# A hybrid gated-mixer block in fp32 on one core: which engine makes the sums of weight quarters

## The chip, the core and the metric

The kernel runs on one core of a Trainium2 chip. Five engines work side by side, each through its own list of instructions in order: TensorE (PE; its weight loads are shown apart as PEld), VectorE (DVE), ScalarE (ACT), GpSimd (POOL) and SyncE (SP). SP issues plain loads. POOL issues loads that add: a DMA that adds what it reads from memory to what lies in a tile. The metric is device microseconds of one execution. The kernel before took 719.77 us (median of 3, 717.58 to 720.23).

## The reference

For x of 512 x 1024, one layer:

```
h = rmsnorm(x, norm_g);  proj = h @ w_in             # w_in: 1024 x 12288
a_u,a_v,a_z, b_p,b_z, c_h,c_b,c_c,c_z, g0,g1,g2 = split(proj, 1024 columns each)
ya = spatial_gating(gelu(a_u), gelu(a_v)) * silu(a_z)
yb = multiscale_pool(b_p) * silu(b_z)                # windows 2, 4, 8, 16, then pool_w
yc = c_b * causal_conv(c_c * c_h, width 3) * silu(c_z)
merged = sum over i of sigmoid(g_i) * (y_i @ w_branch_i)     # three, 1024 x 1024 each
out = rmsnorm(x + merged @ w_out)
```

All of it is in fp32. Almost all the work is in the matrix products with w_in, the three w_branch and w_out.

## The kernel before, in words

**Operands.** Every fp32 operand of a matmul is split in two parts that TensorE multiplies at full rate: ScalarE casts it (`whi`, line 61), VectorE subtracts the cast from it (`wlo`, line 62). Three matmuls (hi·hi, hi·lo, lo·hi) make one product. A tile of weights is 128 x 1024 elements, 512 KB; there are 7 buffers of raw weights (`wraw`), 4 of `whi`, 4 of `wlo`, 2 for a sum that is made by DMA (`wsum`, called `s1`).

**Seven products in place of eight.** A weight block is cut in four quarters and the activations in four too; a scheme of Strassen's kind needs seven products of quarters. For that some operands are sums of weight quarters, and some are sums of activation quarters (`t1` to `t4`, made once at the start; b11, b21, b22 are quarters).

**Groups.** Of the 24 blocks of 512 columns of `w_in`, two are made plainly at the start (line 120 on), and 22 are *groups* (function `group`): two groups for each of the other eleven outputs (`ch`, `cb` and so on; `g` is 0 or 1). A group makes 7 products of 24 matmuls of 256 columns, in the order b11, b21, t2, t1, t3, b22, t4. Its sums of weights: `s1` is one quarter loaded by SP plus another added by POOL (line 460); a11−a21, s1−a11 and a12−(the new a11) are VectorE's (line 448), the second and third each built on an earlier one. `copied` moves a result bank to SBUF (ScalarE), `plus` adds two partial results (VectorE, line 445). The last two products of a group, b22 and t4, are issued after the first product of the next group (`run`, from line 492).

**Projections.** `merge` makes two gate groups and then the projection of a branch: 7 products of 48 matmuls (line 645). Four of its operands lie in turn in one *chain tile*: a quarter, to which POOL adds three more quarters one after the other (`w.add`), each after the product that read the value before it; a fifth load and a fourth adding DMA make `s3`. The output projection (from line 909) is built alike, with matmuls of 512 columns (line 874).

**Order.** A scheduler of the tile framework reorders the instructions of each engine by its own estimate of when operands are ready; so an engine's order isn't that of the code. A buffer is used again when all that reads it is done. Between the groups stand the mixing steps of branch a (line 549), the pooling of branch b (line 747 and `pool_mm`), and the convolution of branch c (ScalarE line 833, VectorE lines 834 and 836), which reads `cc` and stands inside the next group, `cb`.

Of the kernel before, what the change touches and what calls it, by code (L numbers as in the profile page):

```python
# [11 lines left out]
ALU = mybir.AluOpType  # L12
# [4 lines left out]
S = 512  # L17
# [7 lines left out]
PAD = 16  # L25
# [5 lines left out]
def mixers_kernel(ctx, tc, x, norm_g, w_in, sgu_ln_g, sgu_ln_b, sgu_w, sgu_b, pool_w, pool_b, pool_scale,  # L31
# [24 lines left out]
    def bank():  # L56
        return psum.tile([P, 512], F32, tag="ps", name="ps")
# [271 lines left out]
    b11, b12, b22, b21 = hsum  # L329
    moving = {"b11": hq[0, 0], "b21": hq[1, 0], "b22": hq[1, 1]}  # L330

    def sum_form(name, tag, out, in0, in1):
        nc.vector.tensor_tensor(out=out, in0=in0, in1=in1, op=ALU.subtract)
        moving[name] = form_tile(name, tag)
        split(*moving[name], out)


    sum_form("t1", "f3", b11, b12, b11)
    sum_form("t3", "f4", b12, b22, b12)
    sum_form("t2", "f5", b22, b22, b11)  # L340


    ws_bs = outs.tile([P, 2, KT, P], F32, tag="outs", name="ws_bs")
# [45 lines left out]
        nc.vector.tensor_scalar(out=v_t[:, b, :], in0=v_t[:, b, :], scalar1=mv[:, 0:1], scalar2=rv,  # L389
                                op0=ALU.subtract, op1=ALU.mult)  # L390

    sum_form("t4", "f6", b21, b21, b22)

    def proj(w, j, rhs_hi, rhs_lo, nk=KT):
        ps = bank()
# [18 lines left out]
    def pair_of(ap):  # L414
        return ap.rearrange("p (j t) -> p j t", j=2)

    def group(c0, g, ct, use=None):
        def source(kh, nh):
            c = c0 + nh * HALF + g * GC
            return w_in[kh * HALF : (kh + 1) * HALF, c : c + GC].rearrange("(k p) c -> p k c", p=P)  # L420

        def quarter(kh, nh):
            return load_raw(source(kh, nh), [4, GC])

        def halved(raw):
# [12 lines left out]

        def copied(ps):
            s = part.tile([P, S], F32, tag="part", name="part")  # L440
            nc.scalar.copy(out=s, in_=ps)
            return pair_of(s)

        def plus(half, ts, s, ps):
            nc.vector.tensor_tensor(out=ct[:, half, :, ts], in0=pair_of(ps), in1=s, op=ALU.add)  # L445

        def sub(out, in0, in1, op=ALU.subtract):
            nc.vector.tensor_tensor(out=out, in0=in0, in1=in1, op=op)  # L448

        a11 = quarter(0, 0)  # L450
        f = halved(a11)
        px, py, pz = bank(), None, None
        product(f, "b11", px, True)
        yield
        c1 = copied(px)
        a12 = quarter(1, 0)
        f = halved(a12)
        s1 = wsum.tile([P, 4, GC], F32, tag="wsum", name="s1")
        nc.sync.dma_start(out=s1, in_=source(0, 1))
        nc.gpsimd.dma_start(out=s1, in_=source(1, 1), accum_op=ALU.add)  # L460
        a21, a22 = quarter(0, 1), quarter(1, 1)
        py = bank()
        product(f, "b21", py, True)
        plus(0, T1, c1, py)
        sub(a21, a11, a21)
        sub(a11, s1, a11)
        product(halved(a11), "t2", px, False)
        c2 = copied(px)
        pz = bank()
        product(halved(s1), "t1", pz, True)  # L470
        product(halved(a21), "t3", px, False)
        c3 = copied(px)
        sub(a12, a12, a11)
        plus(1, T2, c3, pz)
        yield
        product(halved(a12), "b22", pz, False)
        plus(0, T2, c2, pz)
        if use:
            use(ct[:, 0], 0, slice(0, S))
            use(ct[:, 1, :, T2], 1, T2)  # L480
        product(halved(a22), "t4", px, False)
        if use:
            use(pair_of(px), 1, T1)
        else:
            nc.scalar.copy(out=ct[:, 1, :, T1], in_=pair_of(px))
        yield

    def run(items):
# [21 lines left out]
                    after()  # L510
        finish()

    def act_into(ct, func):
        def use(src, half, ts):
            nc.scalar.activation(out=ct[:, half, :, ts], in_=src, func=func)
        return use

    def y_tile():
# [78 lines left out]
    class Weights:  # L597
# [17 lines left out]
    def parts(raws):  # L615
# [5 lines left out]
            units.append((hi, lo))  # L621
        return units

    def banks():
        return [bank() for _ in range(2)]


    def merge(br, w_branch):
# [49 lines left out]
        def projection():  # L678
            q, w = Quarters(y, home), Weights(w_branch)
            w11 = w.plain(0, 0)  # L680
            px, py = banks(), banks()
            product(w11, q.form("b11"), px, True)
            c1 = copied(px, tile512)
            yield
            chain = w.add(w.plain(1, 0), 1, 1)
            product(w.plain(0, 1), q.form("b21"), py, True)
            under(0, T1, py, c1)
            pz = banks()
            product(chain, q.form("-t1"), pz, True)
            z5 = copied(pz, tile512)  # L690
            w.add(chain, 0, 0)
            product(chain, q.form("-t2"), px, False)
            s3 = w.add(w.plain(0, 0), 1, 0)
            w.add(chain, 0, 1)
            c2 = copied(px, part512)
            product(s3, q.form("t3"), px, False)
            under(1, T2, px, z5, -1.0)
            yield
            product(chain, q.form("b22"), pz, False)
            under(0, T2, pz, c2)  # L700
            product(w.plain(1, 1), q.form("-t4"), px, False)
            under(1, T1, px, None, -1.0)
            yield
# [108 lines left out]
    def branch_c(g):  # L812
        c = {}

        def part_of(name, off, func=None):
            c[name] = out_tile(name)
            yield from group(OFF[off], g, c[name], act_into(c[name], func) if func else None)

        def conv_in():
            c["cc"] = out_tile("cc")  # L820

            def use(src, half, ts):
                nc.vector.tensor_mul(out=pads[half][:, :, PAD + ts.start : PAD + ts.stop], in0=src,
                                     in1=c["ch"][:, half, :, ts])
# [13 lines left out]

        def gate_in():
            c["cb"] = out_tile("cb")  # L840

            def use(src, half, ts):
                y1 = c["cc"][:, half, :, ts]
                nc.vector.tensor_mul(out=y1, in0=src, in1=y1)
# [68 lines left out]
    product(w.plain(0, 0), q.form("b11"), px, True)  # L913
    chain = w.add(w.plain(1, 0), 1, 1)
    product(chain, q.form("-t1"), pz, True)
    w12 = w.plain(0, 1)
    w.add(chain, 0, 0)
# [5 lines left out]
    s3 = w.add(w.plain(0, 0), 1, 0)  # L923
    w.add(chain, 0, 1)
# [4 lines left out]
    product(s3, t3, px, False)  # L929
    w22 = w.plain(1, 1)  # L930
    product(chain, q.form("b22"), pz, False)
# [29 lines left out]
```

## Time and profile before

| | |
|---|---|
| three runs | 717.58, 719.77, 720.23 us |
| the profiled execution | 721.86 us; its span 720.1 us, mean granted TensorE clock 0.983 |
| busy share of the span | PE 95%, PEld 91%, DVE 81%, ACT 53%, POOL 11% |
| HBM read | 118.00 MB, 167 GB/s over the span |
| adding DMAs by POOL (queue software_dynamic) | 28.32 MB |

TensorE is busy nearly throughout, so what can be won or lost in time stands at the few places where it isn't. Its matmuls overlap: one of 256 columns lasts 0.28 us by its row and the next begins 0.117 us later, so time is counted by the distance of their starts. The stages, by the span's clock: start and the first two blocks of `w_in` up to some 99 us, the mixing steps near 100 and 144 us, projection a at 219 to 260, b at 376 to 421, c at 600 to 661, and from there the output projection.

### The profile page before, as it was taken

Reading aid. Unit: us, or ns where it says so; the run is one execution under the profiler, and the core shown is the slowest. Engines: PE = TensorE matmul, PEld = TensorE weight load, DVE = VectorE, ACT = ScalarE, POOL = GpSimd, SP = SyncE. Lnnn points to the kernel's source line nnn. Section 1 sums busy time; section 2 is a strip of 40 time slices with the busy share of each in tenths; the row PEclk is TensorE's granted clock in tenths of the full one; section 3 lists DMA queues with packets and bytes.
Section 4 is the critical chain, followed back from the end, with each engine's and each line's share of the span. In section 5 each row is a group of like instructions: output and inputs, shape, how many; then the busy total and the mean of one; then the engine's idle time right before and its main releaser. Section 6 shows DMA issues by size and latency. Waiting matters only on the chain.

```text
span 720.1 us, 12691 instructions
## 1 busy us (share of the span) xinstructions
PE 684.0 (95%) x5246; PEld 654.7 (91%) x5246; DVE 581.2 (81%) x674; ACT 380.4 (53%) x464; POOL 82.4 (11%) x92
## 2 busy tenths in 40 slices
PE   8999999989998899999998999999999999989694
PEld 6779999989998899999998899999999999989563
DVE  6998678599787798995867797897779896779596
ACT  6544555546454554765764434646445465565253
POOL 3112000000122001000122000000000001212101
PEclk9999999999999999999999999999999999999988
DMA  7964436616689736557598547465666627978833
GB/s 267 326 139 118 147 88 176 176 52 184 177 234 181 180 123 159 149 147 201 139 256 154 151 142 187 151 161 159 150 155 194 176 91 219 244 171 234 184 60 117
DMA packets 96478, 120.93 MB, mean 168 GB/s; under 512 B 3804, under 2 KB 73508, under 8 KB 96420
## 3 DMA queue, kind: packets, MB, share of 16 engines
q1 hardware_dynamic: 75508, 90.75, 39.1%
q0 software_dynamic: 20320, 28.32, 24.0%
q10 hardware_dynamic: 592, 1.05, 0.4%
q8 instruction: 41, 0.67, 0.4%
q14 instruction: 17, 0.14, 0.1%
HBM read 118.00 MB, written 2.10 MB: 167 GB/s over the span
## 4 chain that ended last, share of the span: by engine, by line
PE 69%; DMA 12%; DVE 10%; issue 5%; ACT 2%; POOL 1%; SPq 0%; POOLq 0%; DVEq 0%; ACTq 0%
PE ps L435 53%; PE ps L645 6%; DMA wraw<-in_w_in 4%; DVE wlo L62 3%; PE ps L874 3%; DMA wraw<-in_w_branch_a 3%; DMA wraw<-in_w_branch_b 3%; PE ps L256 2%; DVE win L747 1%; PE ps L97 1%; PE ps L98 1%; PE ps L96 1%; ACT whi L61 1%; DMA wraw<-in_w_out 1%; DMA wraw<-in_w_branch_c 1%
## 5 line engine op out<-in xcount | busy, mean ns | idle before, releaser
L61 ACT CAST whi<-wraw 128x1024 fp32r<-128x1024 f32 (+1 forms) x192 | 199.3, 1041 | 256.1 <-PE ps L435 140.2
L62 DVE TENSOR_TENSOR wlo<-wraw,whi 128x1024 fp32r<-128x1024 f32 (+1 forms) x192 | 231.2, 1210 | 95.4 <-ACT whi L61 95.0
L645 PE MATMUL ps<-yl,whi 128*128 128x256 f32 x336 | 96.6, 288 | 6.4 <-DVE yl L62 6.4
L645 PE MATMUL ps<-yh,wlo 128*128 128x256 f32 x336 | 96.8, 289 | 4.7 <-DVE wlo L62 4.7
L645 PE MATMUL ps<-yh,whi 128*128 128x256 f32 x336 | 96.4, 287 | 0.7 <-ACT yh L61 0.7
L460 POOL DMA_DIRECT2D s<-in_w_in x22 | 28.8, 1310 | 390.1 <-DMA s<-in_w_in 81.3
L645 PEld LDWEIGHTS ps<-yl,whi 128*128 128x128 f32 x336 | 65.3, 194 | 7.2 <-DVE yl L62 7.2
L645 PEld LDWEIGHTS ps<-yh,wlo 128*128 128x128 f32 x336 | 65.5, 195 | 6.1 <-DVE wlo L62 6.1
L645 PEld LDWEIGHTS ps<-yh,whi 128*128 128x128 f32 x336 | 65.4, 195 | 1.1 <-ACT yh L61 1.1
L448 DVE TENSOR_TENSOR wraw<-wraw 128x1024 f32<-128x1024 f32 x44 | 53.5, 1218 | 13.9 <-DMA wraw<-in_w_in 13.8
L435 PE MATMUL ps<-b22h,whi 128*128 128x256 f32 x176 | 51.5, 292 | 3.7 <-DVE sz L445 3.7
L435 PE MATMUL ps<-b22l,whi 128*128 128x256 f32 x176 | 50.0, 284 | 0.0
L435 PE MATMUL ps<-b22h,wlo 128*128 128x256 f32 x176 | 49.8, 283 | 0.0
L435 PE MATMUL ps<-b11l,whi 128*128 128x256 f32 x176 | 49.6, 282 | 0.0
L435 PE MATMUL ps<-t2l,whi 128*128 128x256 f32 x176 | 49.5, 281 | 0.0
L435 PE MATMUL ps<-t1l,whi 128*128 128x256 f32 x176 | 49.5, 281 | 0.0
L435 PE MATMUL ps<-t3l,whi 128*128 128x256 f32 x176 | 49.5, 281 | 0.0
L435 PE MATMUL ps<-b21l,whi 128*128 128x256 f32 x176 | 49.5, 281 | 0.0
L435 PE MATMUL ps<-t4l,whi 128*128 128x256 f32 x176 | 49.5, 281 | 0.0
L435 PE MATMUL ps<-b11h,whi 128*128 128x256 f32 x176 | 49.3, 280 | 0.0
L435 PE MATMUL ps<-t3h,whi 128*128 128x256 f32 x176 | 49.3, 280 | 0.0
L435 PE MATMUL ps<-b21h,whi 128*128 128x256 f32 x176 | 49.3, 280 | 0.0
(243 smaller groups left out, 2002.6 us busy)
## 6 DMA issues: line engine op xcount, KB each, us to landing
wraw<-in_w_in SPq DMA_DIRECT2D x96, 512.0 KB, 4.7
s<-in_w_in SPq DMA_DIRECT2D x22, 512.0 KB, 3.6
s<-in_w_in POOLq DMA_DIRECT2D x22, 512.0 KB, 6.0
wraw<-in_w_branch_a SPq DMA_DIRECT2D x10, 512.0 KB, 6.2
wraw<-in_w_branch_b SPq DMA_DIRECT2D x10, 512.0 KB, 7.2
wraw<-in_w_branch_c SPq DMA_DIRECT2D x10, 512.0 KB, 3.6
wraw<-in_w_out SPq DMA_DIRECT2D x10, 512.0 KB, 8.6
wraw<-in_w_branch_a POOLq DMA_DIRECT2D x8, 512.0 KB, 8.2
```

What stands on the lines that cost most here:

```text
L61: keep(nc.scalar.copy(out=hi, in_=src))
L62: keep(nc.vector.tensor_tensor(out=lo, in0=src, in1=hi.bitcast(F32), op=ALU.subtract))
L96: nc.tensor.matmul(ps, lhsT=a[0], rhs=b[0], start=first, stop=False)
L97: nc.tensor.matmul(ps, lhsT=a[0], rhs=b[1], start=False, stop=False)
L98: nc.tensor.matmul(ps, lhsT=a[1], rhs=b[0], start=False, stop=last)
L256: pin(nc.tensor.matmul(vps[b], lhsT=a, rhs=r, start=done[b] == 1, stop=done[b] == 3 * KT))
L435: nc.tensor.matmul(ps[:, j * GC : (j + 1) * GC], lhsT=a[x][:, k, j * P : (j + 1) * P], rhs=moving[b][y][:, k, :], start=first and j == 0 a ...
L448: nc.vector.tensor_tensor(out=out, in0=in0, in1=in1, op=op)
L460: nc.gpsimd.dma_start(out=s1, in_=source(1, 1), accum_op=ALU.add)
L645: nc.tensor.matmul(ps, lhsT=units[k // 2][x_][:, k % 2, j * P : (j + 1) * P], rhs=form[y_][:, k, :], start=first and j % 2 == 0 and k == 0 ...
L747: nc.vector.tensor_add(out=nxt[:, lo:], in0=cur[:, lo:], in1=cur[:, lo - step : PAD + S - step])
L874: nc.tensor.matmul(pss[b], lhsT=m[x_][:, k, b * P : (b + 1) * P], rhs=units[k // 2][y_][:, k % 2, :], start=first and k == 0 and n == 0, s ...
```

## The change

In a group the products stand in the order b11, b21, −t1, −t2, t3, b22, −t4. The tile `s1` is the operand of −t1 and then, with a11 added to it by VectorE (line 472), of −t2. The tile a11 gets a quarter added by a POOL DMA (line 473) and is the operand of t3. a12 gets `s1` added by VectorE (line 477). No separate tile a21 is loaded; four of six loads stay plain and two add, where it was five and one. The activation sums −t1, −t2 and −t4 have their signs turned, and the operations that read their results take the sign in.

In the projections the chain tile gets one adding DMA, `w11` a second one (two quarters each), and VectorE makes the other two sums (`sum_onto`, line 638 of the changed file), one operation for each half tile. The fifth load and `s3` are gone.

```
def group(...):                     # cut
         a11 = quarter(0, 0)
         product(f, "b11", px, True)
         c1 = copied(px)
-        a12 = quarter(1, 0)
-        f = halved(a12)
         s1 = wsum.tile([P, 4, GC], F32, tag="wsum", name="s1")
         nc.sync.dma_start(out=s1, in_=source(0, 1))
         nc.gpsimd.dma_start(out=s1, in_=source(1, 1), accum_op=ALU.add)
-        a21, a22 = quarter(0, 1), quarter(1, 1)
+        a12 = quarter(1, 0)
+        f = halved(a12)
         py = bank()
         product(f, "b21", py, True)
         plus(0, T1, c1, py)
-        sub(a21, a11, a21)
-        sub(a11, s1, a11)
-        product(halved(a11), "t2", px, False)
-        c2 = copied(px)
-        pz = bank()
-        product(halved(s1), "t1", pz, True)
-        product(halved(a21), "t3", px, False)
+        pz = bank()
+        product(halved(s1), "-t1", pz, True)
+        nc.vector.tensor_tensor(out=s1, in0=s1, in1=a11, op=ALU.add)
+        nc.gpsimd.dma_start(out=a11, in_=source(0, 1), accum_op=ALU.add)
+        product(halved(s1), "-t2", px, False)
+        c2 = copied(px)
+        a22 = quarter(1, 1)
+        nc.vector.tensor_tensor(out=a12, in0=a12, in1=s1, op=ALU.add)
+        product(halved(a11), "t3", px, False)
         c3 = copied(px)
-        sub(a12, a12, a11)
-        plus(1, T2, c3, pz)
+        plus(1, T2, c3, pz, 1.0 if use else -1.0)
         yield
         product(halved(a12), "b22", pz, False)
...
+    def sum_onto(raws, others):
+        for a, b in zip(raws, others):
+            nc.vector.tensor_tensor(out=a, in0=a, in1=b, op=ALU.add)
...
def projection():                   # cut
             chain = w.add(w.plain(1, 0), 1, 1)
-            product(w.plain(0, 1), q.form("b21"), py, True)
-            under(0, T1, py, c1)
+            w12 = w.plain(0, 1)
             pz = banks()
             product(chain, q.form("-t1"), pz, True)
+            sum_onto(chain, w11)
+            w.add(w11, 1, 0)
             z5 = copied(pz, tile512)
-            w.add(chain, 0, 0)
+            py = banks()
+            product(w12, q.form("b21"), py, True)
+            under(0, T1, py, c1)
             product(chain, q.form("-t2"), px, False)
-            s3 = w.add(w.plain(0, 0), 1, 0)
-            w.add(chain, 0, 1)
             c2 = copied(px, part512)
-            product(s3, q.form("t3"), px, False)
+            sum_onto(w12, chain)
+            product(w11, q.form("t3"), px, False)
             under(1, T2, px, z5, -1.0)
             yield
-            product(chain, q.form("b22"), pz, False)
+            product(w12, q.form("b22"), pz, False)
```

The output projection changes in the same way. The orders of the engines move with it; three places follow, before and then after. A name's number tells its tile.

VectorE in the first group after projection b (`ch`, g = 0), from the split of its first tile on, before: `pr` and `merged` belong to the projection, `s1_4644` is the group's `s1`, `wraw_4605` its a11, `wraw_4638` its a12, `wraw_4647` its a21, `part` a copied bank.

```order
L62 TENSOR_TENSOR wlo_4608<-wraw_4605,whi_4607 128x1024
L62 TENSOR_TENSOR wlo_4641<-wraw_4638,whi_4640 128x1024
L661 TENSOR_TENSOR pr_4597<-ps_4053,gate_3537 128x512
L448 TENSOR_TENSOR wraw_4605<-s1_4644,wraw_4605 128x1024
L662 TENSOR_TENSOR merged_2472<-merged_2472,pr_4597 128x2x256
L661 TENSOR_TENSOR pr_4600<-ps_4054,gate_3883 128x512
L62 TENSOR_TENSOR wlo_4680<-wraw_4605,whi_4679 128x1024
L662 TENSOR_TENSOR merged_2472<-merged_2472,pr_4600 128x2x256
L62 TENSOR_TENSOR wlo_4711<-s1_4644,whi_4710 128x1024
L62 TENSOR_TENSOR wlo_4739<-wraw_4647,whi_4738 128x1024
L445 TENSOR_TENSOR ch_4604<-ps_4651,part_4636 128x2x256
L448 TENSOR_TENSOR wraw_4638<-wraw_4638,wraw_4605 128x1024
```

The same place after: `s1_4606` is `s1`, `wraw_4573` a11, `wraw_4609` a12, `wraw_4737` the a11 of the next group.

```order
L62 TENSOR_TENSOR wlo_4612<-wraw_4609,whi_4611 128x1024
L678 TENSOR_TENSOR merged_2529<-merged_2529,pr_4565 128x2x256
L677 TENSOR_TENSOR pr_4568<-ps_4026,gate_3857 128x512
L62 TENSOR_TENSOR wlo_4643<-s1_4606,whi_4642 128x1024
L678 TENSOR_TENSOR merged_2529<-merged_2529,pr_4568 128x2x256
L472 TENSOR_TENSOR s1_4606<-s1_4606,wraw_4573 128x1024
L477 TENSOR_TENSOR wraw_4609<-wraw_4609,s1_4606 128x1024
L451 TENSOR_TENSOR ch_4572<-ps_4615,part_4604 128x2x256
L62 TENSOR_TENSOR wlo_4673<-s1_4606,whi_4672 128x1024
L62 TENSOR_TENSOR wlo_4706<-wraw_4573,whi_4705 128x1024
L62 TENSOR_TENSOR wlo_4740<-wraw_4737,whi_4739 128x1024
L62 TENSOR_TENSOR wlo_4769<-wraw_4609,whi_4768 128x1024
```

The split of `s1` (for −t1) now stands ahead of the sum into `s1`; the split of a11 (for t3, `wraw_4573`) stands behind it and behind a DMA, and the split of the next group's first tile right behind that one.

VectorE in the first `cb` group, around the convolution, before: `ppad` is its padded input, lines 834 and 836 the convolution, `wraw_4995` the group's s1−a11 (t2), `s1_5106` its t1, `wraw_5109` its t3.

```order
L62 TENSOR_TENSOR wlo_5142<-wraw_4995,whi_5141 128x1024
L448 TENSOR_TENSOR wraw_5335<-wraw_5233,wraw_5335 128x1024
L445 TENSOR_TENSOR cc_4770<-ps_4933,part_4931 128x2x256
L62 TENSOR_TENSOR wlo_5173<-s1_5106,whi_5172 128x1024
L823 TENSOR_TENSOR ppad0_1780<-cc_4770,ch_4604 128x2x512
L823 TENSOR_TENSOR ppad1_1782<-ps_4777,ch_4604 128x2x256
L62 TENSOR_TENSOR wlo_5201<-wraw_5109,whi_5200 128x1024
L834 SCALAR_TENSOR_TENSOR cc_4770<-ppad0_1780,pvec_451,cc_4770 128x512 x2
L836 SCALAR_TENSOR_TENSOR cc_4770<-ppad0_1780,pvec_451,cc_4770 128x512 x2
L834 SCALAR_TENSOR_TENSOR cc_4770<-ppad1_1782,pvec_451,cc_4770 128x512 x2
L836 SCALAR_TENSOR_TENSOR cc_4770<-ppad1_1782,pvec_451,cc_4770 128x512 x2
L445 TENSOR_TENSOR cb_4994<-ps_5113,part_5098 128x2x256
```

The same place after: `s1_5064` holds −t1's operand up to line 472 and −t2's from there, and lines 851 and 853 are the convolution.

```order
L472 TENSOR_TENSOR s1_5064<-s1_5064,wraw_4959 128x1024
L477 TENSOR_TENSOR wraw_5067<-wraw_5067,s1_5064 128x1024
L451 TENSOR_TENSOR cc_4736<-ps_4863,part_4922 128x2x256
L523 SCALAR_TENSOR_TENSOR ppad1_1772<-ps_4743,ch_4572 128x2x256
L521 TENSOR_TENSOR ppad0_1770<-cc_4736,ch_4572 128x2x512
L851 SCALAR_TENSOR_TENSOR cc_4736<-ppad1_1772,pvec_451,cc_4736 128x512 x2
L851 SCALAR_TENSOR_TENSOR cc_4736<-ppad0_1770,pvec_451,cc_4736 128x512 x2
L853 SCALAR_TENSOR_TENSOR cc_4736<-ppad0_1770,pvec_451,cc_4736 128x512 x2
L853 SCALAR_TENSOR_TENSOR cc_4736<-ppad1_1772,pvec_451,cc_4736 128x512 x2
L451 TENSOR_TENSOR cb_4958<-ps_5073,part_5062 128x2x256
L62 TENSOR_TENSOR wlo_5131<-s1_5064,whi_5130 128x1024
L62 TENSOR_TENSOR wlo_5164<-wraw_4959,whi_5163 128x1024
```

Three splits of the group stood ahead of the convolution; now the two sums stand ahead of it, and the splits of −t2 and t3 behind it.

TensorE at the end of −t2 in the first `ch` group, after (`ps_4579` is the group's bank, `ps_4743` one of the next group, 12 matmuls of which stand here):

```order
L439 MATMUL ps_4579<--t2h_442,whi_4672 128x256
L439 MATMUL ps_4579<--t2l_443,whi_4672 128x256
L439 MATMUL ps_4579<--t2h_442,wlo_4673 128x256
L439 MATMUL ps_4743<-b11h_169,whi_4739 128x256
L439 MATMUL ps_4743<-b11l_170,whi_4739 128x256
L439 MATMUL ps_4743<-b11h_169,wlo_4740 128x256
```

And the end of those 12 matmuls:

```order
L439 MATMUL ps_4743<-b11h_169,whi_4739 128x256
L439 MATMUL ps_4743<-b11l_170,whi_4739 128x256
L439 MATMUL ps_4743<-b11h_169,wlo_4740 128x256
L439 MATMUL ps_4579<-t3h_437,whi_4705 128x256
L439 MATMUL ps_4579<-t3l_438,whi_4705 128x256
```

Before, t2, t1 and t3 of one group followed each other; the border of t1 and t3 (`ps_4709` is the other bank of the group):

```order
L435 MATMUL ps_4709<-t1h_432,whi_4710 128x256
L435 MATMUL ps_4709<-t1l_433,whi_4710 128x256
L435 MATMUL ps_4709<-t1h_432,wlo_4711 128x256
L435 MATMUL ps_4611<-t3h_437,whi_4738 128x256
L435 MATMUL ps_4611<-t3l_438,whi_4738 128x256
L435 MATMUL ps_4611<-t3h_437,wlo_4739 128x256
L435 MATMUL ps_4611<-t3h_437,whi_4738 128x256
```

After, matmuls of the next group's b11 stand ahead of t3, so that TensorE reaches that tile's split before t3's.

## Rows read from the trace of the kernel before

**Rows 1.** The page's first part: busy us (share of the span) and instructions.

```profile
PE 684.0 (95%) x5246; PEld 654.7 (91%) x5246; DVE 581.2 (81%) x674; ACT 380.4 (53%) x464; POOL 82.4 (11%) x92
```

**Rows 2.** Windows: us, PE, PEld, DVE, ACT, POOL busy (x), PEclk, DMA share, GB/s.

```profile
99.10:106.00 6.90, 6.15 (x52) 5.96 (x52) 6.90 (x12) 2.01 (x3) 0.00 (x0) 1.00 0.01 2
143.51:153.50 9.99, 7.21 (x50) 7.02 (x50) 8.88 (x13) 2.74 (x3) 0.26 (x2) 0.83 0.01 3
218.78:259.82 41.04, 36.68 (x290) 35.67 (x289) 30.39 (x33) 18.62 (x22) 4.80 (x4) 0.96 0.71 168
376.21:421.46 45.25, 40.19 (x316) 38.92 (x315) 35.79 (x42) 19.36 (x23) 4.80 (x4) 0.96 0.63 150
600.00:661.00 61.00, 58.68 (x485) 58.27 (x484) 44.45 (x49) 33.30 (x39) 10.80 (x9) 0.97 0.89 223
660.90:710.60 49.70, 41.73 (x170) 31.94 (x168) 39.83 (x51) 21.47 (x32) 8.15 (x7) 0.93 0.53 115
500.00:520.00 20.00, 20.00 (x171) 19.86 (x170) 16.24 (x16) 9.90 (x12) 1.29 (x1) 1.00 0.61 160
```

**Rows 3.** The chain of waits: start us, us, engine and what.

```profile
136.80 7.73 DMA wraw<-in_w_in
...
673.93 8.89 DMA wraw<-in_w_out
...
694.74 13.49 PE ps L874 x57
```

**Rows 4.** Windows, after the wait of projection a.

```profile
248.00:252.00 4.00, 4.00 (x22) 4.00 (x23) 3.48 (x6) 0.00 (x0) 0.00 (x0) 0.57 0.61 171
```

**Rows 5.** Waits: engine, line, waited for: us in total, times, longest us.

```profile
ACT whi L61 <- DMA wraw<-in_w_branch_a: 9.4, 3, 7.9
...
DVE wraw L448 <- DMA wraw<-in_w_in: 3.2, 1, 3.2
...
PE ps L874 <- ACT mh L61: 7.1, 1, 7.1
```

**Rows 6.** Groups by form: busy, mean ns of one, idle before.

```profile
L62 DVE TENSOR_TENSOR wlo<-wraw,whi 128x1024 fp32r<-128x1024 f32 x188 | 228.5, 1221 | 94.2 <-ACT whi L61 93.8
L61 ACT CAST whi<-wraw 128x1024 fp32r<-128x1024 f32 x188 | 196.8, 1050 | 250.1 <-PE ps L435 134.2 <-issue 32.0 <-PE ps L645 20.7
...
L448 DVE TENSOR_TENSOR wraw<-s,wraw 128x1024 f32<-128x1024 f32 x22 | 26.9, 1221 | 0.3
```

**Rows 7.** DMA issues: KB each, median us to landing; then line 460 alone.

```profile
s<-in_w_in SPq DMA_DIRECT2D x22, 512.0 KB, 3.6
s<-in_w_in POOLq DMA_DIRECT2D x22, 512.0 KB, 6.0
...
wraw<-in_w_branch_a POOLq DMA_DIRECT2D x8, 512.0 KB, 8.2
...
DMA to landing us min/median/max: 5.5/6.0/11.8
```

**Rows 8.** Timeline of VectorE: start us, us, engine, line, operation.

```profile
464.00 1.41 DVE L834 SCALAR_TENSOR_TENSOR cc<-ppad,pvec,cc 128x512 f32<-128x512 f32 x2
...
469.90 3.49 DVE L62 TENSOR_TENSOR wlo<-wraw,whi 128x1024 fp32r<-128x1024 f32 x3
```

**Rows 9.** Timeline of TensorE and ScalarE at a product's end.

```profile
441.06 0.28 PE L435 MATMUL ps<-t4h,wlo 128*128 128x256 f32 x1
...
441.26 1.05 ACT L61 CAST whi<-wraw 128x1024 fp32r<-128x1024 f32 x1 [1.67 <-PE ps L435]
...
442.21 0.58 ACT L485 COPY ch<-ps 128x512 f32<-128x512 f32 x1
```

**Rows 10.** Timeline of VectorE and POOL, projection a.

```profile
218.00 1.22 DVE L62 TENSOR_TENSOR wlo<-wraw,whi 128x1024 fp32r<-128x1024 f32 x1
...
219.53 1.19 POOL L612 DMA_DIRECT2D wraw<-in_w_branch_a  x1 [2.77 <-DVE wlo L62]
```

**Rows 11.** Timeline of ScalarE, the convolution's activations.

```profile
462.38 2.94 ACT L833 ACTIVATE cc<-ppad,pvec 128x512 f32<-128x512 f32 x4
```

More of the change, by code (lines that the diff above doesn't have):

```diff
@@ L330, in mixers_kernel, with sum_form @@
     moving = {"b11": hq[0, 0], "b21": hq[1, 0], "b22": hq[1, 1]}
-    def sum_form(name, tag, out, in0, in1):
-        nc.vector.tensor_tensor(out=out, in0=in0, in1=in1, op=ALU.subtract)
+    def sum_form(name, tag, out, in0, in1, sign=1.0):
+        if sign == 1.0:
+            nc.vector.tensor_tensor(out=out, in0=in0, in1=in1, op=ALU.subtract)
+        else:
+            nc.vector.scalar_tensor_tensor(out=out, in0=in0, scalar=sign, in1=in1, op0=ALU.mult, op1=ALU.subtract)
         moving[name] = form_tile(name, tag)
         split(*moving[name], out)
-    sum_form("t1", "f3", b11, b12, b11)
+    sum_form("-t1", "f3", b11, b11, b12)
     sum_form("t3", "f4", b12, b22, b12)
-    sum_form("t2", "f5", b22, b22, b11)
+    sum_form("-t2", "f5", b22, b22, b11, -1.0)
     ws_bs = outs.tile([P, 2, KT, P], F32, tag="outs", name="ws_bs")
@@ L390, in mixers_kernel @@
                                 op0=ALU.subtract, op1=ALU.mult)
-    sum_form("t4", "f6", b21, b21, b22)
+    sum_form("-t4", "f6", b21, b22, b21, -1.0)
     def proj(w, j, rhs_hi, rhs_lo, nk=KT):
@@ L442, in copied, with plus @@
             return pair_of(s)
[L444 to L448, printed above, removed]
+        def plus(half, ts, s, ps, sign=1.0):
+            o = ct[:, half, :, ts]
+            if sign == 1.0:
+                nc.vector.tensor_tensor(out=o, in0=pair_of(ps), in1=s, op=ALU.add)
+            else:
+                nc.vector.scalar_tensor_tensor(out=o, in0=pair_of(ps), scalar=sign, in1=s, op0=ALU.mult,
+                                               op1=ALU.subtract)
         a11 = quarter(0, 0)
         f = halved(a11)
-        px, py, pz = bank(), None, None
+        px = bank()
         product(f, "b11", px, True)
@@ L478, in group @@
         if use:
-            use(ct[:, 0], 0, slice(0, S))
-            use(ct[:, 1, :, T2], 1, T2)
-        product(halved(a22), "t4", px, False)
+            use(ct[:, 0], 0, slice(0, S), 1.0)
+            use(ct[:, 1, :, T2], 1, T2, -1.0)
+        product(halved(a22), "-t4", px, False)
         if use:
-            use(pair_of(px), 1, T1)
+            use(pair_of(px), 1, T1, -1.0)
         else:
-            nc.scalar.copy(out=ct[:, 1, :, T1], in_=pair_of(px))
+            nc.scalar.mul(out=ct[:, 1, :, T1], in_=pair_of(px), mul=-1.0)
         yield
@@ L511, in run, with times, use @@
         finish()
+    def times(out, in0, in1, sign):
+        if sign == 1.0:
+            nc.vector.tensor_mul(out=out, in0=in0, in1=in1)
+        else:
+            nc.vector.scalar_tensor_tensor(out=out, in0=in0, scalar=sign, in1=in1, op0=ALU.mult, op1=ALU.mult)
     def act_into(ct, func):
-        def use(src, half, ts):
-            nc.scalar.activation(out=ct[:, half, :, ts], in_=src, func=func)
+        def use(src, half, ts, sign):
+            nc.scalar.activation(out=ct[:, half, :, ts], in_=src, func=func, scale=sign)
         return use
@@ L680, in projection @@
             w11 = w.plain(0, 0)
-            px, py = banks(), banks()
+            px, py, pz = banks(), None, None
             product(w11, q.form("b11"), px, True)
@@ L820, in conv_in, with use @@
             c["cc"] = out_tile("cc")
-            def use(src, half, ts):
-                nc.vector.tensor_mul(out=pads[half][:, :, PAD + ts.start : PAD + ts.stop], in0=src,
-                                     in1=c["ch"][:, half, :, ts])
+            def use(src, half, ts, sign):
+                times(pads[half][:, :, PAD + ts.start : PAD + ts.stop], src, c["ch"][:, half, :, ts], sign)
             yield from group(OFF["cc"], g, c["cc"], use)
@@ L840, in gate_in, with use @@
             c["cb"] = out_tile("cb")
-            def use(src, half, ts):
+            def use(src, half, ts, sign):
                 y1 = c["cc"][:, half, :, ts]
-                nc.vector.tensor_mul(out=y1, in0=src, in1=y1)
+                times(y1, src, y1, sign)
             yield from group(OFF["cb"], g, c["cb"], use)
@@ L912, in mixers_kernel @@
     px, pz = banks(), banks()
-    product(w.plain(0, 0), q.form("b11"), px, True)
+    w11 = w.plain(0, 0)
+    product(w11, q.form("b11"), px, True)
     chain = w.add(w.plain(1, 0), 1, 1)
+    w12 = w.plain(0, 1)
     product(chain, q.form("-t1"), pz, True)
-    w12 = w.plain(0, 1)
-    w.add(chain, 0, 0)
+    sum_onto(chain, w11)
+    w.add(w11, 1, 0)
     b21 = q.form("b21")
@@ L922, in mixers_kernel @@
     product(chain, q.form("-t2"), px, False)
-    s3 = w.add(w.plain(0, 0), 1, 0)
-    w.add(chain, 0, 1)
+    sum_onto(w12, chain)
     onto(1, 1, pz, ALU.subtract)
@@ L928, in mixers_kernel @@
     onto(1, 0, px, ALU.add)
-    product(s3, t3, px, False)
+    product(w11, t3, px, False)
     w22 = w.plain(1, 1)
-    product(chain, q.form("b22"), pz, False)
+    product(w12, q.form("b22"), pz, False)
     onto(1, 1, px, ALU.subtract, last=True)
```

## The prediction

> **What bounds the kernel now.** I read five views in this order. The page's first part: TensorE is busy for 95% of the span, VectorE for 81% [rows 1]. So time can go only where TensorE waits, and the next engine has little room. Then the windows, cut at product borders, to see where TensorE waits [rows 2]. In the long stretch of `w_in` groups it issues 171 matmuls of 256 columns in 20.0 us, 0.117 us each, and nothing can be won there. Against that pitch six places lose time: after the two mixing steps 0.8 us (6.9 − 52×0.117) and 4.1 us (10.0 − 50×0.117); in the projection of branch a 7.1 (41.0 − 290×0.117), of b 8.3 (45.25 − 316×0.117), of c 4.3 (61.0 − 485×0.117); in the output projection 9.9 (49.7 − 168×0.237, the pitch of a full-rate 512-column run in [rows 3]). Together 34.5 us, with what the clock takes: after the wait of projection a the granted clock was 0.57 for 4 us, the lower of its two levels for most of that time, and that alone cost 1.7 us [rows 4]. The chain of waits and the wait table name the reasons: a load that VectorE's sum waits for while the result that TensorE needs stands behind it, and adding DMAs that follow each other in the chain tile [rows 3, 5].
>
> **What goes.** In a projection the chain tile now gets one adding DMA instead of three; its other two sums, and the loads `s3`, are gone. Each of the two sums is two operations on VectorE, one for each half tile (1.2 us each [rows 6]), beside TensorE. The second adding DMA goes into `w11`, two products (11 us) before it is needed, against 8.2 us of landing [rows 7]: hidden. So the waits in a, b and c go, less what VectorE's four added sums (4.6 us a projection at the back-to-back pitch of 1.14 us [rows 8]) bring: I count rows against products and find 0.5, 0.6 and 1.0 us left. Gains 6.6, 7.7 and 3.3. In the output projection the wait of 7 us before the third product goes, but VectorE then has, between the start of the second product and the fifth, 23.4 us of rows for 16.9 us of matmuls, so the fifth waits some 5.5: gain 9.9 − 5.5 = 4.4. After the mixing steps, no VectorE sum waits for a fresh load any more: gain 4.9. Sum of gains 26.9 us. All of it is bounded by the measured loss, from 0 to 34.5.
>
> Elsewhere: VectorE loses 22 sums and gets 16, −7 us of busy time that stands beside TensorE; loads fall by 12 MB, and the queues were not what TensorE waited for in the group stretch. The negated forms replace one operation by another of the same shape: nothing. Cover for all this is a matmul stream of 0.117 us; where that is gone I price it below.
>
> **What comes.** In every `w_in` group the third sum, `a11`, is now made by an adding DMA that may start only when VectorE has added `a11` into `s1`; and that sum writes `s1` in place, so it follows the split of −t1. The path is: a buffer of `whi` comes free when the fourth last product ends; 0.2 us later ScalarE casts (1.05 us) [rows 9]; VectorE forms `wlo` (1.2), then the sum (1.15); POOL issues 0.3 us after VectorE [rows 10]; the DMA lands 6.0 us after issue (5.5 at best [rows 7]); cast 1.1, `wlo` of t3 1.2, and behind it `wlo` of the next group's b11 1.15, since VectorE's order has it second while TensorE's order has 13 (or 12) matmuls of that b11 first, ahead of t3. From the end of `wlo`(−t1) this is 1.15+0.3+6.0+1.1+1.2+1.15 = 10.9 us. TensorE can issue two of these matmuls, the third needs that `wlo`.
> In the usual group `wlo`(−t1) ends 2.95 us after the buffer's release, ready at 13.85. TensorE has 120 matmuls from there, needed at 14.5: no wait, 0.7 us to spare.
> Six groups have no b22 and t4 of an earlier group between their b11 and b21. After projection b: need 0.1+4×2.82+0.3 = 11.7; VectorE still merges, so the sum starts at 4.1, ready 15.0: wait 3.3. After projection a: sum starts at 3.65, wait 2.8. After the two pool products: need 14.2, but two operations that wait for the last pool product, −t1's split and one more split stand ahead of the sum, ready 17.4: 3.2 each. After the two mixing steps: need 13.5, two products into `y` (1.14 each) stand ahead of the sum, ready 15.6, and the smaller cover before b22 costs 0.7: 2.8 each. Together 18.1 us.
> The two groups that carry a convolution lose in another way. Before, three splits stood ahead of its eight VectorE operations (0.66 us each) and TensorE ran on; now the split of −t2 stands behind all of them and behind ScalarE's four activations [rows 8, 11]. I follow the rows from the release of the buffer: sum done 4.8, the last plus before the convolution 6.5, convolution done 13.5, plus 14.1, `wlo`(−t2) 15.3, needed at 11.7. Wait 3.6 each, 7.2 us.
> Small ones: t3 now follows −t2 on the same bank and waits for a copy that stands behind a cast, 0.2 + 0.95 + 0.58 = 1.75 us after −t2's last matmul, of which 13 matmuls cover 1.65; the same before t4: 0.1 us a group, 2.3 in all. The pool rows ahead of projection a's first split: 0.7. Sum 3.0.
> A wait of 3 us was followed by the lower clock in one place, while one of 1.0 us was not [rows 2]. Eight new waits are about that long; I charge half of them 1.7 us (10.0 us × 0.17, what the window with that fall lost): 6.8, with ends of 0 and 13.6.
> Sum: −26.9 + 18.1 + 7.2 + 3.0 + 6.8 = +8.2 us.
>
> [...] [rows 7] show 6.0 us for an adding DMA of 512 KB. [...]
>
> **Rivals.** (1) Faster: the adding DMA costs no wait. The place is the third sum in the six groups; it decides at a landing of about 3 us, where ready meets need (6.0 less the 2.8 to 3.3 of wait). A plain load of the same tile lands in 3.6 us [rows 7], and I take that as the lower bound. Then 18.1 falls by 6×2.4 to 3.7 and the clock's charge by 5.1 (six of the eight waits): 728 − 20 = 708. For it: less traffic, and TensorE may be later than I count. Against: the minimum of 22 landings.
> (2) Gains and losses cancel: no lower clock after the new waits, 728 − 7 = 721; with a landing of 5.5, 718.
> (3) The projections don't give their waits back, because VectorE is the limit there (its share was already 30.4 of 41.0 us in a [rows 2], and 4.6 us are added): half of 17.6 us is lost, 728 + 9 = 737. Against: the rows that are late can wait for the next group.
> (4) The adding DMA lands as in the projections, 8.2 us, in all groups: the usual group then waits 1.5 us (12×1.5 = 18), the six 2.2 more (13): 759. Against: the queues are less full there, a DMA share of 0.61 in the group stretch against 0.71 in projection a [rows 2].
> That the change doesn't do what it says is excluded by the order: the waits stand where I place them.
>
> **How the numbers follow.** The sum is made on the profiled execution, 721.86 us, span 720.1. It lies 2.1 us above the median of 719.77. 721.9 + 8.2 = 730.1, minus 2.1: 728. Chances: forecast 0.46 (its own range 722 to 740), rival 1 0.24, rival 2 0.13, rival 3 0.11, rival 4 0.06. The range 703 to 742 leaves out rival 4, the upper part of 3 and the best of 1. Half a per cent is 3.6 us, about what a measurement of this kernel can tell from no change: faster below 716.2, slower above 723.4. Faster 0.25 (rival 1, a little of 2), same 0.14, slower 0.61.
>
> **What would show it.** In the new profile: TensorE's waits for VectorE's `wlo` of `wraw` in the first group after projections a and b of about 3 us, with ScalarE waiting there for a DMA into `wraw` from `w_in` by POOL; a wait of 3 to 4 us for `wlo` of `s` in the two convolution groups; no wait of ScalarE for a branch's adding DMA; one wait near 5 us late in the output projection; the usual group at 20.0 us still. I am wrong if the six groups show no wait (rival 1), or if the usual group's period grows by over 0.5 us (rival 4).

## The result, and the profile after

The changed kernel took 751.12 us (median of 4, 748.87 to 752.92), the kernel before 719.99 beside it: a ratio of 1.044 (95% interval 1.040 to 1.048). It is slower, as forecast, by nearly four times the forecast amount (8 us), and above the range of 703 to 742. The profiled executions differ by 27.0 us (748.87 against 721.86; spans 747.1 and 720.1), and these 27 us are what the traces can explain. One execution of the kernel with the groups alone, the profiled one, was a slow one (774 us; the other three took 761.6 to 765.8), so its time below is the median of those three, and of its trace only what POOL issued is used.

The page's first part, against [rows 1]:

```profile
PE 698.3 (93%) x5246; PEld 664.2 (89%) x5246; DVE 573.8 (77%) x668; ACT 377.7 (51%) x464; POOL 90.2 (12%) x98
```

TensorE and VectorE both have a smaller share of a longer span; TensorE's idle time grew from 36 to 49 us, and its mean granted clock is 0.973 where it was 0.983. The windows that answer to [rows 2] (us, busy time of PE, PEld, DVE, ACT, POOL, then PEclk, DMA share, GB/s) are in this order: behind the two mixing steps, the group between them, the last gate group ahead of projection a, projections a and b, the last gate group ahead of c, the first convolution, a usual group, the output projection:

```profile
101.36:107.30 5.94, 5.94 (x51) 5.81 (x50) 5.56 (x9) 3.39 (x4) 0.00 (x0) 1.00 0.27 91
149.46:155.40 5.94, 5.94 (x51) 5.81 (x50) 5.56 (x9) 3.39 (x4) 0.25 (x2) 1.00 0.38 105
116.00:128.00 12.00, 9.79 (x68) 9.38 (x67) 4.63 (x4) 5.04 (x6) 1.30 (x1) 0.86 0.82 202
208.38:232.59 24.21, 19.91 (x146) 19.41 (x145) 15.96 (x24) 12.40 (x15) 2.48 (x2) 0.86 0.49 113
232.59:266.51 33.92, 33.92 (x290) 33.92 (x289) 32.20 (x35) 19.19 (x23) 1.22 (x1) 1.00 0.55 147
394.49:428.40 33.91, 33.91 (x291) 33.91 (x290) 33.64 (x40) 18.24 (x22) 1.20 (x1) 1.00 0.59 155
613.20:639.95 26.75, 24.98 (x194) 24.43 (x193) 19.77 (x19) 15.29 (x18) 3.70 (x3) 0.94 0.66 158
480.00:491.00 11.00, 8.16 (x65) 7.55 (x64) 10.45 (x13) 5.11 (x6) 0.69 (x1) 1.00 0.43 119
530.07:550.35 20.28, 20.28 (x170) 19.92 (x169) 11.79 (x12) 9.21 (x11) 2.59 (x2) 1.00 0.66 155
691.66:737.10 45.44, 40.89 (x168) 32.01 (x166) 43.01 (x55) 21.04 (x31) 4.31 (x4) 0.96 0.25 61
```

Projection a takes 33.92 us for 290 matmuls where it took 41.04; the same 0.117 us a matmul holds in b, and behind the mixing steps nothing is lost. The loss is in the other windows: 24.2 us for 146 matmuls ahead of projection a (17.1 at that pitch), 12.0 for 68 (8.0), 11.0 for 65 (7.6).

Both kernels issue 5246 matmuls in nearly the same order, so the n-th matmul of one can be set against the n-th of the other, and the growth of the lag shows where the time went. Beside it what the prediction had for the place (the waits without the 6.8 us for the clock):

| place | lag grows by, us | predicted |
|---|---|---|
| start, before the first group | +1.8 | 0 |
| behind the mixing steps | −4.5 | −4.9 |
| projections a, b, c | −7.2, −8.3, −4.4 | −6.6, −7.7, −3.3 |
| output projection, with c's last product | −1.7 | −4.4 |
| the six groups | +4.3, +4.2, +2.9, +5.5, +2.7, +5.2 | +18.1 in all |
| the two convolution groups | +4.3, +5.4 | +7.2 in all |
| last gate group ahead of projection a | +7.8 | +0.7 |
| last gate group ahead of projection c | +5.7 | 0 |
| first group of branch c's second half | +1.1 | 0 |
| all else | +1.6 | +2.3 |

The mechanism in one of the six groups, the one of the window 116:128; timelines of VectorE, ScalarE, POOL and TensorE (start us, us, what, idle before and releaser):

```profile
110.02 1.22 DVE L472 TENSOR_TENSOR s<-s,wraw 128x1024 f32<-128x1024 f32 x1
...
119.07 4.63 DVE L62 TENSOR_TENSOR wlo<-wraw,whi 128x1024 fp32r<-128x1024 f32 x4 [4.83 <-ACT whi L61]
...
117.99 3.89 ACT L61 CAST whi<-wraw 128x1024 fp32r<-128x1024 f32 x4 [5.67 <-DMA wraw<-in_w_in]
...
111.88 1.29 POOL L473 DMA_DIRECT2D wraw<-in_w_in  x1 [16.61 <-ACT part L445]
...
120.03 0.38 PE L439 MATMUL ps<-b11h,whi 128*128 128x256 f32 x1 [1.26 <-ACT whi L61]
120.26 0.28 PE L439 MATMUL ps<-b11l,whi 128*128 128x256 f32 x1
121.48 0.38 PE L439 MATMUL ps<-b11h,wlo 128*128 128x256 f32 x1 [0.95 <-DVE wlo L62]
```

VectorE adds into `s1` at 110.0, POOL issues 0.64 us behind that sum, the DMA lands 6.1 us later at 117.98, ScalarE casts t3's tile, then the next b11's, and VectorE splits them in that order, while TensorE wants b11 first: two matmuls, then a second wait. This is the path of the prediction. Soon after it the matmuls followed each other at 0.21 us for 3.4 us at a granted clock of 0.50 (122.4 to 125.8), and the window's granted clock is 0.86; the engine had waited 1.26 and 0.95 us.

### The profile page after: what moved, and what is told of

It reads as the page before. It is cut to its first block, busy times and chain, and to the rows that moved or that the text cites. A ratio compares the mean times of both kernels' runs of the same rounds, so it can differ in the third digit from the quotient of the medians.

```text
span 747.1 us, 12625 instructions
## 1 busy us (share of the span) xinstructions
PE 698.3 (93%) x5246; PEld 664.2 (89%) x5246; DVE 573.8 (77%) x668; ACT 377.7 (51%) x464; POOL 90.2 (12%) x98
## 3 DMA queue, kind: packets, MB, share of 16 engines
q0 software_dynamic: 27584, 31.46, 26.8%
## 5 line engine op out<-in xcount | busy, mean ns | idle before, releaser
L62 DVE TENSOR_TENSOR wlo<-wraw,whi 128x1024 fp32r<-128x1024 f32 (+1 forms) x170 | 201.1, 1206 | 140.6 <-ACT whi L61 140.6
L61 ACT CAST whi<-wraw 128x1024 fp32r<-128x1024 f32 (+1 forms) x170 | 171.3, 1037 | 236.2 <-PE ps L439 97.1
L61 ACT CAST whi<-s 128x1024 fp32r<-128x1024 f32 x44 | 46.2, 1051 | 50.0 <-PE ps L439 36.6
L473 POOL DMA_DIRECT2D wraw<-in_w_in x22 | 28.5, 1294 | 281.8 <-DVE s L472 214.3
L439 PE MATMUL ps<-b11h,wlo 128*128 128x256 f32 x176 | 52.0, 295 | 5.6 <-DVE wlo L62 5.6
L62 DVE TENSOR_TENSOR wlo<-s,whi 128x1024 fp32r<-128x1024 f32 x44 | 53.6, 1218 | 0.8 <-ACT whi L61 0.8
L439 PE MATMUL ps<--t2h,wlo 128*128 128x256 f32 x176 | 49.9, 283 | 3.3 <-DVE wlo L62 3.3
L439 PE MATMUL ps<-t3h,wlo 128*128 128x256 f32 x176 | 51.4, 292 | 0.0
L439 PE MATMUL ps<--t4h,whi 128*128 128x256 f32 x176 | 51.2, 291 | 0.0
L439 PE MATMUL ps<--t2l,whi 128*128 128x256 f32 x176 | 50.0, 284 | 0.0
```

What stands on the lines that cost most here:

```text
L61: keep(nc.scalar.copy(out=hi, in_=src))
L62: keep(nc.vector.tensor_tensor(out=lo, in0=src, in1=hi.bitcast(F32), op=ALU.subtract))
L473: nc.gpsimd.dma_start(out=a11, in_=source(0, 1), accum_op=ALU.add)
```

## Experiments

**The projections alone.** Groups as before; `projection`, `sum_onto` and the output projection as changed.

> The groups as before, the projections and the output projection as changed. Theory G (all of the loss is made in the groups, and the projections give back what their steps in the comparison of the two traces show: 7.2, 8.3, 4.4 and 1.7 us): 720.0 - 21.6 = 698 us. Rival P (the waits of 7.4 us ahead of projection a and 5.7 us ahead of projection c come from the changed projections, whose adding DMAs stand ahead of the groups' own in POOL's list): 698 + 13 = 711 us, with those two waits still there.

Measured: 702.8 us, ratio 0.977 (0.975 to 0.979). Theory G holds for the place of the loss; of its 21.6 us, 17.2 came. Against the kernel before, the lag falls by 7.0 us in a, 6.4 in b, 4.1 in c and 3.5 in the output projection, 2.1 behind the second mixing step, and grows by over 0.9 us nowhere but at c's last product (1.8). The waits ahead of projections a and c aren't there, so they need the changed groups.

**The groups alone.** The changed kernel with both kinds of projections as before.

> The groups as changed, the projections and the output projection as before. Theory G: 751.1 + 21.6 = 773 us, waits of TensorE ahead of t3 in the same groups as in the changed kernel. Rival P: 773 - 13 = 760 us, with no wait of over 2 us ahead of projections a and c.

Measured: 763.5 us, ratio 1.062 (1.058 to 1.065). Between the two: the groups cost 43.5 us by themselves, the projections give back 12.4 here (763.5 to 751.1) and 17.2 with the old groups. POOL's list has the old projection's adding DMAs ahead of the last gate group's third sum as well, which was issued 0.3 us after the first of them had landed (207.95 and 208.22). So that wait needs the changed groups, not the changed projection, and rival P's reason falls, though its number (760) is nearer than theory G's (773); what the projections gave less by was not traced.

**The third sum on VectorE.**

```diff
-        nc.gpsimd.dma_start(out=a11, in_=source(0, 1), accum_op=ALU.add)
+        nc.vector.tensor_tensor(out=a11, in0=a11, in1=a21, op=ALU.add)   # a21 = quarter(0, 1)
```

> The changed kernel, but the third sum of a group is made by VectorE from a plain load of the fourth quarter, in place of the adding DMA behind the sum into s1. Theory D (TensorE waits in the groups for the chain sum, adding DMA, cast, split): the eight group waits without the convolution's (24 us), the 7.4 and 5.7 us ahead of projections a and c, and most of the lower clock go: 751 - 36 = 715 us, and with the mixing steps and projections as they are perhaps 705. Rival V (VectorE's order is what costs: the sums stand behind the split of -t1 and ahead of that of -t2): the waits stay, and 22 operations of 1.22 us more on VectorE make it 751 us or more.

Measured: 719.6 us, ratio 0.998 (0.996 to 1.001): 31.5 us less than the changed kernel with 22 more VectorE operations of 1.2 us. Theory D holds, rival V falls. What it left is not small: two waits of 3.41 us ahead of −t2 at the convolution, one of 1.4 ahead of projection a.

**The adding DMA early.**

```diff
-        nc.gpsimd.dma_start(out=a11, in_=source(0, 1), accum_op=ALU.add)
+        a21 = quarter(0, 0)          # loaded behind a12
+        nc.gpsimd.dma_start(out=a21, in_=source(0, 1), accum_op=ALU.add)
...
-        product(halved(a11), "t3", px, False)
+        product(halved(a21), "t3", px, False)
```

> The changed kernel, but the third sum of a group is made by an adding DMA into a tile of its own that is loaded a second time, so that it does not wait for VectorE's sum into s1: as many adding DMAs, 11.5 MB more of plain loads. Theory D: as in the kernel with VectorE's sum, 705 to 715 us, since the DMA starts a product or more earlier. Rival Q (two adding DMAs in each group are too many for POOL's queue, whatever they wait for): no better than 740 us, with landings of 7 us and more and ScalarE waiting for them.

Measured: 717.3 us, ratio 0.996 (0.994 to 0.998). As many adding DMAs as in the changed kernel and more loads, yet 34 us less. TensorE's waits in the groups for a cast or a split, in the changed kernel and then here (in all us, times, longest us):

```profile
PE ps L439 <- ACT whi L61: 10.4, 7, 2.2
PE ps L439 <- DVE wlo L62: 8.9, 8, 1.8
```

```profile
PE ps L439 <- DVE wlo L62: 6.3, 2, 3.1
```

The two that are left are the convolution's, 3.41 us between two starts each. So the cost is not the adding DMA, but that it starts only behind a VectorE sum that waits itself. The time is 2 us above the upper end of theory D, which had left the convolution's waits standing; what these 2 us are was not traced. Not tried was the late DMA as it is, with the next b11's cast and split put ahead of t3's, so how much of the loss is due to that order is open.

**More room for POOL's adding DMAs.** `dynamic_dma_scratch_size`, the room meant here, from 2048 to 3072, nothing else.

> The changed kernel with its room for the descriptors of POOL's DMAs raised from 2048 to 3072 bytes, every engine's order unchanged. Theory R (an adding DMA of 512 descriptors behind two of 256, or behind one of 512, is issued only when the first of them has landed: 0.3 us after it in the three places ahead of the projections and in several groups): ahead of projections a and c the third sum is issued within 0.7 us of VectorE's sum, 3 us earlier, the landing is unchanged, and the time is 751 - 8 = 743 us. Rival (POOL waits there for the VectorE operation that the profile names as the releaser): no change, 751 us, and the issue at the same distance behind the sum.

Measured: 745.8 us, ratio 1.039 (1.034 to 1.043). Ahead of projection a, POOL in the changed kernel and then with more room:

```profile
198.85 1.20 POOL L624 DMA_DIRECT2D wraw<-in_w_branch_a  x1 [8.04 <-DVE ppad L453]
200.26 1.20 POOL L624 DMA_DIRECT2D wraw<-in_w_branch_a  x1 [0.21 <-issue]
204.75 1.30 POOL L473 DMA_DIRECT2D wraw<-in_w_in  x1 [3.29 <-DVE win L765]
```

```profile
197.94 1.19 POOL L624 DMA_DIRECT2D wraw<-in_w_branch_a  x1 [8.40 <-DMA wraw<-in_w_branch_a]
199.34 1.22 POOL L624 DMA_DIRECT2D wraw<-in_w_branch_a  x1 [0.21 <-issue]
200.07 1.82 POOL L473 DMA_DIRECT2D wraw<-in_w_in  x1
```

The third one no longer waits, so "DVE win" was a releaser only by coincidence in time: in the changed kernel the first of the pair landed 5.6 us after its issue, at 204.45, and the third was issued 0.3 us later. But with more room it landed 11.3 us after its issue, at 211.4, where it had landed at 204.75 + 7.5 = 212.25: TensorE's wait ahead of projection a stayed (3.74 and 1.56 us between two starts, 3.25 and 1.75 in the changed kernel). Room alone is not the answer there. The issue was as theory R had it; its time came out near the figure, but not at the place named, and as far as the traces show by luck. They differ by 3.6 us, and three steps of 1.5 to 1.9 us lie where the changed kernel's trace has the granted clock at 0.50 (122.4 to 125.8, 573.0 to 576.4, 627.6 to 631.0) and this one has 1.00. The intervals of the two ratios overlap (1.034 to 1.043 and 1.040 to 1.048), so a gain is not shown.

**The order of POOL's list.** Both kinds of adding DMAs kept in the order of the program (`pin` is the scheduler's keep_in_program_order); no other engine's order changes.

```diff
-        nc.gpsimd.dma_start(out=a11, in_=source(0, 1), accum_op=ALU.add)
+        pin(nc.gpsimd.dma_start(out=a11, in_=source(0, 1), accum_op=ALU.add))
...
-                nc.gpsimd.dma_start(out=raw, in_=self.source(n, k, u), accum_op=ALU.add)
+                pin(nc.gpsimd.dma_start(out=raw, in_=self.source(n, k, u), accum_op=ALU.add))
```

> The changed kernel with POOL's adding DMAs kept in the order of the program: the third sum of the last gate group ahead of each projection is issued before that projection's own adding DMAs, not behind them; the other engines' orders are unchanged. Theory Q (ahead of projections a and c the third sum is late because it is served behind two adding DMAs of the projection; more room alone only issued it earlier and it landed as late): it lands about 6 us after its issue, so 5 us earlier, TensorE's waits of 3.7 and 1.6 us ahead of projection a go with the lower clock behind them, and the time is 751 - 8 = 743 us. Rival (VectorE's pooling operations are what is late there, and the projection's chain becomes late in its turn): 751 us, with waits of the same size at -t1 of the projections.

Measured: 744.6 us, ratio 1.035 (1.031 to 1.039). POOL and ScalarE at the same place:

```profile
200.02 1.29 POOL L473 DMA_DIRECT2D wraw<-in_w_in  x1 [10.42 <-DVE s L472]
200.77 1.76 POOL L624 DMA_DIRECT2D wraw<-in_w_branch_a  x1
206.25 1.22 POOL L624 DMA_DIRECT2D wraw<-in_w_branch_a  x1 [3.72 <-issue]
```

```profile
205.96 2.95 ACT L61 CAST whi<-wraw 128x1024 fp32r<-128x1024 f32 x3 [3.74 <-DMA wraw<-in_w_in]
```

The third sum now lands at 200.02 + 5.9, 6 us earlier; ahead of projection a one wait of 1.31 us is left, the granted clock stays at 1.00 (204 to 230), and the lag at that place is 5.7 us smaller. That settles 5.7 of the 7.8 us ahead of a: two adding DMAs of the projection were served first. Ahead of c theory Q holds for the smaller part alone: a wait of 0.93 us at t3 is gone, but the one of 2.05 us at b22 is one of 2.07 now. VectorE's timeline of this kernel shows why; it runs without a pause up to and past the sum of two partial results (`gate`, 624.22) that TensorE, by the profile, waits for until 624.96:

```profile
611.97 1.23 DVE L62 TENSOR_TENSOR wlo<-wraw,whi 128x1024 fp32r<-128x1024 f32 x1 [1.83 <-ACT whi L61]
613.87 1.23 DVE L62 TENSOR_TENSOR wlo<-wraw,whi 128x1024 fp32r<-128x1024 f32 x1 [0.68 <-ACT whi L61]
615.01 1.22 DVE L62 TENSOR_TENSOR yl<-y,yh 128x1024 fp32r<-128x1024 f32 x1
...
621.94 1.22 DVE L583 SCALAR_TENSOR_TENSOR y<-y 128x1024 f32<-128x1024 f32 x1
623.08 1.22 DVE L62 TENSOR_TENSOR wlo<-wraw,whi 128x1024 fp32r<-128x1024 f32 x1
624.22 0.68 DVE L451 TENSOR_TENSOR gate<-ps,part 128x512 f32<-128x512 f32 x1
```

```profile
624.96 0.39 PE L439 MATMUL ps<-b22h,whi 128*128 128x256 f32 x1 [1.80 <-DVE gate L451]
```

The pause in front of that run (1.83 and 0.68 us; t3's cast had waited 3.26 us for its DMA) is time that VectorE lacks behind it, where it also makes the projection's activation sums. That this pause is the whole cause was not tried by itself; with the early DMA the wait is gone.

**The convolution later.** Its operations are issued behind the next group's first five products, in the changed kernel and in the one with the early DMA.

```diff
-                    done()
+                    held.append(done) if done.__name__ == "conv" else done()
...
                 next(gen)
+                while held:
+                    held.pop()()
```

> The changed kernel with the convolution's operations issued after the next group's first five products in the program, so that on VectorE they stand behind the splits of -t2 and t3. Theory C (the two waits of 3.4 us ahead of -t2, and 1 us of lower clock behind each, are the convolution standing ahead of the split): 751 - 9 = 742 us. Rival (the eight operations of 0.67 us delay whichever split stands behind them, so the wait moves to b22 or the next b11): 751 us.

> The kernel with the early adding DMA into a tile of its own, and the convolution issued later as well. Theory C: 717 - 9 = 708 us, with no wait of over 1 us in the groups but the one ahead of projection a. Rival as before: 717 us.

Measured: 748.4 us on the changed kernel, ratio 1.039 (1.034 to 1.044), near the rival; its interval overlaps that of the changed kernel. At the first convolution the waits of 1.62 and 1.77 us at −t2 went and one of 2.15 us ahead of t3 came. It is not for t3's split, which ended at 486.70, but for the copy of the bank that −t2 filled and t3 adds to. On ScalarE that copy stands behind three casts, and those behind t3's cast, which waited for its DMA (the last line is TensorE's):

```profile
484.39 1.05 ACT L61 CAST whi<-wraw 128x1024 fp32r<-128x1024 f32 x1 [2.54 <-DMA wraw<-in_w_in]
...
486.77 2.93 ACT L61 CAST whi<-wraw 128x1024 fp32r<-128x1024 f32 x3
489.60 0.57 ACT L445 COPY part<-ps 128x512 f32<-128x512 f32 x1
...
490.22 0.39 PE L439 MATMUL ps<-t3h,whi 128*128 128x256 f32 x1 [1.87 <-ACT part L445]
```

On the early DMA it was 708.3 us, ratio 0.985 (0.982 to 0.989), 9.0 us less, as theory C had it in time. But a part of the waits moved here too, against its "no wait of over 1 us": in place of 3.41 us at −t2, each convolution has 1.55 us ahead of t3, again for that copy. Several late things stood at one place, and taking away one showed the next.

**The order before, with two VectorE sums.** What the runs pointed to: an early DMA for t3, −t2's operand made in a11 so that it does not wait for −t1's split, and −t1 back between −t2 and t3.

```diff
+        a21, a22 = quarter(0, 0), quarter(1, 1)
+        nc.gpsimd.dma_start(out=a21, in_=source(0, 1), accum_op=ALU.add)
...
+        nc.vector.tensor_tensor(out=a11, in0=s1, in1=a11, op=ALU.add)
+        product(halved(a11), "-t2", px, False)
...
+        product(halved(s1), "-t1", pz, True)
+        nc.vector.tensor_tensor(out=a12, in0=a12, in1=a11, op=ALU.add)
+        product(halved(a21), "t3", px, False)
```

> Groups in the order before (b11, b21, -t2, -t1, t3), VectorE making two sums of which none waits for the split of -t1, the third sum by an early adding DMA into a tile of its own; the projections as changed. Theory D (what costs is only what waits behind the sum into s1, and the small waits of 0.13 us where t3 follows -t2 on one bank): no waits in the groups, no wait of VectorE for a load behind the mixing steps, so the 703 us of the kernel with the projections alone, less 3: 700 us. Rival Q2 (three adding DMAs where two stood take POOL's queue past its room: each is issued 6 us or more behind the one before): waits of ScalarE for the third sum, 708 us or more.

Measured: 697.1 us, ratio 0.968 (0.966 to 0.971), the fastest of all; the projections alone gave 0.977. Its first part, and the window of [rows 2]'s group stretch:

```profile
PE 677.6 (97%) x5246; PEld 650.7 (94%) x5246; DVE 574.9 (83%) x668; ACT 380.0 (55%) x464; POOL 90.0 (13%) x98
```

```profile
500.00:520.00 20.00, 20.00 (x171) 19.86 (x170) 13.89 (x14) 9.72 (x12) 2.59 (x2) 1.00 0.75 173
```

VectorE has 13.9 us of work in 20 where it had 16.2, at the same pitch of TensorE, and no wait of TensorE in a group exceeds 0.45 us. It has as many adding DMAs as the changed kernel and none of the waits that rival Q2 named, so Q2 falls.

## Why the prediction was wrong

**What goes: right.** The gains sum to 26.1 us in the table, 26.9 predicted. The output projection kept the wait before its fifth product: 3.88 us between two starts, then 0.51, 1.13 and 0.59, some 5.2 us above the pitch, for 5.5 predicted. What came short is at c's last product, a new wait of 1.56 us.

**What comes, at the places named: right in kind, a little low.** The path of the adding DMA was the mechanism, its landing 5.7 us (median of 22, 5.6 at best) where 6.0 was taken, its issue 0.64 us behind the sum in the group shown where 0.3 was taken. Six groups and two convolutions grew by 34.5 us, 18.1 + 7.2 + 6.8 for the clock = 32.1 predicted. All else, the copies between −t2 and t3 among it, grew by 1.6 for the 2.3 of the "small ones".

**The step that failed is the list of places, "Six groups have no b22 and t4 of an earlier group between".** I looked for groups with too little cover and left the adding DMA's landing the same everywhere. Ahead of projection a the cover is there, but POOL's list has the projection's two adding DMAs ahead of the group's third sum, which then landed 11.3 us behind VectorE's sum (200.97 to 212.25) in place of 6.4; I priced that border at 0.7 us and it cost 7.8. The order of POOL's list showed it, and I priced the issue of DMAs and not their service one after another. With POOL's order turned, 5.7 of the 7.8 us went. Ahead of projection c 5.7 us were missed. Of these 1.4 stand at t3, and some 3.6 at b22, with a granted clock of 0.50 behind that wait (627.6 to 631.0); b22's is most likely due to VectorE's pause. The start lost 1.8 that I had not looked at: TensorE waits there 0.97 us for the load of `ws_bs`, which SP issued 0.8 us later than before; this was not tried apart. With 1.1 us in branch c, whose cause was not looked for, these are 15.7 of the 18.4 us between +8.2 and +26.6.

**The rivals.** Rival 1 needed a landing of 3 us; no adding DMA landed in under 5.5 in the traces before and after. Rival 3 was wrong: the projections are at 0.117 us with VectorE busy for 95% of a's window and 99% of b's. Rival 4 came nearest in time (759) by a mechanism that is half right: a third sum that arrives late, in the groups ahead of projections a and c and not in all. The usual group grew by 0.3 us, not 1.5. Rivals 1 to 3 all had the groups beside a projection at the same price, so the range ended 9 us too low.

**The rest.** The profiled execution has no fixed place among the runs: I took 2.1 us off to come to the median, and here the median lies 2.3 us above it.

## What to carry to other kernels

In this kernel a sum that moved from an engine to an adding DMA was cheap only where the DMA could start early (717.3 us against 751.1). So price the whole path from the last instruction it waits for to the last one that waits for it, and give it a tile of its own if that lets it start a product sooner. Ask of each adding DMA not only what it waits for but what stands ahead of it in its issuer's list, above all where two stages meet. When two waits stand at one place, removing one only shows the other, so test them together too.

## What the runs showed of the hardware

POOL's adding DMAs met a limit here. With `dynamic_dma_scratch_size` at 2048, one of 512 pieces of 1 KB (a quarter of `w_in`) did not start behind two of 256 pieces of 2 KB (halves of a branch's quarter) until the first had landed: the issue came 0.3 us after the landing (204.45 and 204.75; 631.46 and 631.75). In both these places the profile puts the wait down to a VectorE operation that ended just then. In the kernel before, one of 512 behind one of 512 was issued in the same way (landing 41.73, issue 42.03). One of 512 and one of 256 went together (with POOL's list in order issued at 200.02 and 200.77, the first landing at 205.9), and with 3072 so did two of 256 and one of 512 (197.94, 199.34 and 200.07); these three then landed one after another, at 203.8, 207.1 and 211.4. What the setting counts in, no run shows. The profile's table has the adding DMAs in one queue, software_dynamic (27584 packets and 31.46 MB in the changed kernel, 22528 of the packets of 1 KB and 4096 of 2 KB).

TensorE's granted clock was 1.00 or 0.50 in the traces before and after, and waits of nearly one size were followed by either. Near 120 us there were 1.54 and 1.23 us between two starts in the changed kernel, and from 122.4 to 125.8 the granted clock was 0.50; with POOL's list in order there were 1.39 and 1.23, and it was 1.00 in the same stretch. At the first convolution of the changed kernel there were 1.62 and 1.77, and from 480 to 491 it was 1.00.
